# Half of the first output projection in seven-product groups, and two more gate groups behind the last attention head

## The chip, the cores and the metric

The kernel runs on one core of a Trainium2 chip. The time is the device time of one execution of the whole program in microseconds (us); lower is better. The core has a matrix engine (TensorE, PE in the views; its weight loads are listed as PEld), a vector engine (DVE), a scalar engine (ACT), GpSimd (POOL), and the SyncE queue (SP), which here only issues DMAs. ACT and POOL issue some DMAs too. The engines take their own instructions in the order of the program and wait for each other through semaphores.

## The reference

Two transformer blocks in a row on 512 tokens of width 2048, in float32. The part that the change touches is the end of the first block:

```python
zin = rmsnorm(x, gain) @ w_in
q, k, v, g_attn, u, g_pool, m_attn, m_pool = split(zin)
o_attn = stick_breaking_attention(q, k, v) * silu(g_attn)      # 8 heads of 128
o_pool = (multiscale_pool(u) @ pool_w) * pool_scale * silu(g_pool)
merged = sigmoid(m_attn) * (o_attn @ w_attn_up) + sigmoid(m_pool) * (o_pool @ w_pool_up)
hs = x + merged @ w_out                                        # 2048 x 2048
x1 = rmsnorm(hs, final_gain)                                   # enters the second block
```

The second block has two layers, each with sliding-window attention, latent attention and an output projection onto a residual; its first layer begins with a norm of x1.

## The kernel before

**Number format.** Every float32 operand is split into two parts, high and low, in a format that TensorE takes at full rate. A product is three matmuls: high by high, high by low, low by high. Weights come by DMA as chunks of 128x1024 into six buffers `ws`; `ahead` (L175) splits a chunk with one ACT copy (`wh`, L195) and one DVE subtraction (`wl`, L196), up to two chunks ahead of the matmuls.

**Plain units.** `unit` (L380) makes one output tile (128 features x 512 tokens) from its chunks; a chunk is 8 contraction tiles, so 24 matmuls of 512 columns. The up projections `w_au` and `w_pu` take one chunk for each of 16 output tiles, the output projection `w_out` takes two for each of 16. An evacuation function then reads the finished PSUM bank; for `w_out` that is `ev_out` (L837), which adds the residual (read from `xT`), scales by the final gain, stores the tile in DRAM (`xs`), splits it for the next block, and adds its squares to two sums on POOL.

**Groups.** Most of the first block's input projection runs in groups (`products`, L235). A group makes two output tiles from four chunks, and treats weights and tokens as 2x2 blocks, so that seven products p1, p2, q5, p3, p6, p7, q4 do the work of eight. Each product is 24 matmuls of 256 columns (272 where the 16 meta tokens go along) into one of three PSUM regions ga, gb, gc. The sums of weight chunks are made by accumulating DMAs, issued by POOL (L204), three in a group, and one DVE addition (L202); the sums of token blocks are made once, in tiles that stay in SBUF (`XS`). `expand` (L215) writes the order: the last three products p3, p7, q4 of a group run inside the next one; before a `Flush` mark a group ends by itself.

**Heads.** The plan runs over 8 heads. Head h has a group for query and gate and one for key and value. Behind the even heads come a group for pool gates and one for pool inputs, behind the odd ones three "gate groups" (`gate_group`, L767: the merge gates m_attn, m_pool, whose sigmoids are written to DRAM, `smd`, by ACT's queue). Twelve gate groups in all. The attention of a head is a generator (`stick`, L897): pieces of it are issued between the matmuls of later groups. When a piece may come is set by an estimated clock that counts matmuls only: each `yield cost, delay, banks` says after how much estimated time (ns) the next piece may go, and `poll` (L122) lets it in. At its end the generator transposes the values on PE (`pv`, L1000), has ACT and DVE split them (`vh`, L1003, `vl`, L333), waits `yield 5 * 109, 3500, 1` (L1010), and then issues the 15 matmuls `o` (L1019) into the same PE stream. The result goes to DRAM (`oad`).

**Order around the last head.** `reload` (L751) brings attention outputs back from `oad` as tiles `rh`, `rl`: tiles 0 to 2 ahead of the last gate group, tiles 3 to 7 in `attention_done` (L787), which first issues what is left of all generators. Then follow the `w_au` units, whose first one reads all eight tiles. All general tiles share a pool of 77 buffers. SP issues weight loads, reloads and stores in program order.

**Second block.** In its first layer `pre_x` (L1297) loads the residual tiles `xr` one unit ahead and scales each by `rs1` on POOL (L1303).

Of the kernel before, what the change touches and what calls it, by code (L numbers as in the profile page):

```python
# [14 lines left out]
P = 128  # L15
D = 2048
KT = D // P
S = 512
# [50 lines left out]

class Group:  # L70


    def __init__(self, blocks, X, evacs, cols, meta=0):
        self.b, self.X, self.evacs, self.cols, self.meta = blocks, X, evacs, cols, meta


class K:
# [137 lines left out]
    def expand(self, plan):  # L215

        out, left, mid = [], [], []
        for n, u in enumerate(plan):
            if isinstance(u, Group):
                p1, p2, q5, p3, p6, p7, q4 = self.products(u)  # L220
                x3, x7, x4 = [[x] for x in left] or ([], [], [])
                if isinstance(plan[n + 1], Flush):
# [12 lines left out]
    def products(self, g):  # L235
# [7 lines left out]
        st = {}  # L243
# [12 lines left out]
        def product(key, op, region, first, after):  # L256
            c0, c1 = (mid, hi) if op in ("A22", "S1", "S3") else (lom if key in ("p1", "p2", "p3", "p6") else lo, mid)

            def body():
                wh, wl = self.chunk()  # L260
                if first:
                    st[region] = self.bank("g" + region)
                o = st[region][:, c0 - lom:c1 - lom] if c0 < mid else st[region][:, lo - lom:mid - lom]
                mm = nc.tensor.matmul
                nj = len(g.X)
                for part in range(2):
                    for n in range(nj):
                        xh, xl, oh, ol = g.X[n][op]
                        xh, xl = xh[:, oh + c0:oh + c1], xl[:, ol + c0:ol + c1]
                        sl = slice(n * P, n * P + P)  # L270
                        if part == 0:
                            mm(o, wh[:, sl], xh, start=first and n == 0, stop=False, skip_group_check=True)  # L272
                            mm(o, wh[:, sl], xl, start=False, stop=False, skip_group_check=True)  # L273
                        else:
                            mm(o, wl[:, sl], xh, start=False, stop=n == nj - 1, skip_group_check=True)  # L275
                        if n % 4 == 3 or part == 0 and n % 2:
                            yield 4 * 118
                after(st[region])
# [3 lines left out]
        wide = slice(0, mid - lom)  # L282
# [3 lines left out]
        main = slice(lo - lom, mid - lom)  # L286

        def after1(a):
            st["y0"], st["y1"] = self.U("y0"), self.U("y1")
            nc.scalar.copy(st["y0"][:, two], a[:, main])  # L290
            if g.meta:
                nc.scalar.copy(st["y0"][:, hi:hi + g.meta], a[:, :g.meta])

        def after2(a):
            nc.scalar.copy(st["y0"][:, one], a[:, wide])

        def after5(c):
            nc.vector.tensor_tensor(st["y1"][:, two], c[:, main], st["y0"][:, two], ALU.subtract)

        def after6(b):  # L300
            y = st["y1"]
            nc.vector.tensor_tensor(y[:, lo:mid], b[:, main], st["y0"][:, two], ALU.add)
            if g.meta:
                nc.vector.tensor_tensor(y[:, lom:lo], b[:, :g.meta], st["y0"][:, hi:hi + g.meta], ALU.add)

        def after3(c):
            v = st["y1"][:, one]
            nc.vector.tensor_tensor(v, c[:, wide], v, ALU.subtract)

        def after7(b):  # L310
            w = st["y1"][:, two]
            nc.vector.tensor_tensor(w, w, b[:, main], ALU.subtract)  # L312
            g.evacs[1](st["y1"])

        def after4(b):
            nc.vector.tensor_tensor(st["y0"][:, two], b[:, main], st["y0"][:, two], ALU.add)
            g.evacs[0](st["y0"])
# [160 lines left out]
    def build(self):  # L478
        nc, tc, i = self.nc, self.tc, self.i
        with tc.tile_pool(name="cst", bufs=1) as cp, tc.tile_pool(name="wp", bufs=1, reuse_waits="tile") as self.wp, \  # L480
# [16 lines left out]
            self.oad = [self.dp.tile([8, P, S], F32, name=f"oad{n}") for n in range(2)]  # L497
            self.opd = [self.dp.tile([8, P, S], F32, name=f"opd{n}") for n in range(2)]
# [10 lines left out]
    def block1(self, plan):  # L509
# [4 lines left out]
        def load():  # L514
# [27 lines left out]
            def sums():  # L542
# [15 lines left out]
                nc.vector.tensor_scalar(self.trir[:, P:], self.ones, -1.0, None, ALU.mult)  # L558
                yield from self.rms_gen(acc, NT, D, self.rsb, 5000, True)
# [37 lines left out]
        X = self.X  # L597
        XS = self.XS = []
# [152 lines left out]
        def reload(dst, src, ts):  # L751
            def f():
                for t in ts:
                    h, l = dst[t] = self.UR("rh"), self.UR("rl")
# [17 lines left out]
        for g in range(4):  # L772
# [3 lines left out]
            rest.append([x for _ in range(3) for x in gate_group(next(ms_))])  # L776
        rest[7].insert(2, reload(self.oa, self.oad, range(3)))
# [38 lines left out]
        ms = []  # L816

        def ev_yp(n):
            def f(b):
# [5 lines left out]
                h, l = self.UR("mh"), self.UR("ml")  # L825
                self.split(h[:, :S], l[:, :S], t[:, :S])
                ms.append((h, l))
                merged[n] = None
            return f
# [5 lines left out]
        acc = {}  # L835

        def ev_out(n):  # L837
            def f(b):
                if n == 0:
                    self.op.clear()  # L840
                    acc[0], acc[1] = self.U("acc1"), self.U("acc2")
                xr, hs, fg = xres.pop(n), self.U("hs"), self.U("fgx")
                nc.vector.tensor_tensor(hs[:, :S], b, xr[:, :S], ALU.add)
                nc.scalar.activation(fg[:, :S], hs[:, :S], AF.Copy, scale=self.vcol(V_FG, n))
                nc.sync.dma_start(self.xs[0][n], fg[:, :S])
                h, l = self.UR("xh"), self.UR("xl")
                g = self.vcol(V_G0, n)
                nc.scalar.activation(h[:, :S], fg[:, :S], AF.Copy, scale=g)
                nc.vector.scalar_tensor_tensor(l[:, :S], fg[:, :S], g, h[:, :S].bitcast(F32), ALU.mult, ALU.subtract)
                for a, t in ((0, hs), (1, fg)):  # L850
                    sq = self.U("sq")
# [825 lines left out]
```

## Time and profile before

| | |
|---|---|
| runs of the kernel | 2661.83, 2662.19, 2663.93 us; median 2662.19 us |
| the profiled execution | 2662.2 us |
| its span (first to last instruction) | 2660.5 us |
| granted TensorE clock, mean | 0.991 of full |
| PE busy | 2607.5 us, 98% of the span |
| DVE, ACT, POOL busy | 1634.5 us (61%), 1255.3 us (47%), 592.0 us (22%) |

The page gives busy times, the span in 40 slices, the DMA queues, the chain of work that ended last and the costliest groups of instructions. Matmuls overlap, so the time that one adds is the distance from its start to the next one's start, not its own duration. All times in the views are us from the start of the span.

### The profile page before, as it was taken

The page shows a single profiled execution, that of the slowest core. Times are in us where ns is not written, and L with a number is a line of the kernel's source. Part 1 is how long each engine was busy: PE and PEld are TensorE (multiplying, and loading weights), DVE is VectorE, ACT ScalarE, POOL GpSimd, SP SyncE. Part 2 cuts the span into 40 slices and gives each one's busy share as a digit, 9 for nine tenths or more (in the row PEclk, how much of TensorE's full clock was granted, in tenths as well). Part 3 has the DMA queues.
Part 4 walks back from the last instruction along what each step waited for, and adds up shares of the span by engine and source line. Part 5 has one row for each costly group of instructions (what it writes and reads, how often), then busy time and mean ns, then how long its engine had stood idle before and what let it go on. Part 6 is the DMA issues. An engine that isn't in the chain of part 4 may idle for free.

```text
span 2660.5 us, 38650 instructions
## 1 busy us (share of the span) xinstructions
PE 2607.5 (98%) x15038; PEld 2286.7 (86%) x15038; DVE 1634.5 (61%) x2285; ACT 1255.3 (47%) x2195; POOL 592.0 (22%) x664
## 2 busy tenths in 40 slices
PE   8999999999999899999999999999999999999997
PEld 7899999999999878888888888888888888888886
DVE  7667767767767634644566655567455665556734
ACT  6655655654655522233345544444334554434433
POOL 2121122123123100022113321243211332113223
PEclk9999999999999999999999999999999999999998
DMA  5567767776776764444322223323332222232322
GB/s 196 159 157 188 199 166 194 190 172 167 186 182 171 191 237 147 143 138 143 115 97 81 72 80 106 94 74 115 120 124 90 80 76 83 95 105 74 104 95 72
DMA packets 117721, 351.05 MB, mean 132 GB/s; under 512 B 12833, under 2 KB 17441, under 8 KB 117537
## 3 DMA queue, kind: packets, MB, share of 16 engines
q1 hardware_dynamic: 90592, 273.06, 30.8%
q0 software_dynamic: 15552, 56.63, 12.4%
q10 hardware_dynamic: 11392, 18.88, 1.9%
q8 instruction: 118, 1.93, 0.3%
q14 instruction: 67, 0.54, 0.1%
HBM read 319.16 MB, written 29.36 MB: 131 GB/s over the span
## 4 chain that ended last, share of the span: by engine, by line
PE 79%; DVE 6%; ACT 6%; issue 4%; DMA 3%; POOL 1%; ACTq 0%; SPq 0%; DVEq 0%; POOLq 0%
PE pm L353 38%; PE pm L361 19%; ACT wh L195 2%; DVE wl L196 2%; PE s L1534 2%; DMA ws<-w_in 2%; PE gb L272 2%; PE gb L273 2%; PE gb L275 2%; PE ga L275 2%; PE gc L272 1%; PE gc L273 1%; PE gc L275 1%; PE ga L272 1%; PE ga L273 1%
## 5 line engine op out<-in xcount | busy, mean ns | idle before, releaser
L196 DVE TENSOR_TENSOR wl<-ws,wh 128x1024 fp32r<-128x1024 f32 (+3 forms) x549 | 703.3, 1284 | 390.7 <-ACT wh L195 386.1
L195 ACT CAST wh<-ws 128x1024 fp32r<-128x1024 f32 (+3 forms) x549 | 561.3, 1030 | 248.7 <-PE pm L353 110.8
L353 PE MATMUL pm<-xh,wh 128*128 128x512 f32 x1120 | 445.5, 398 | 8.2 <-ACT xh L532 7.5
L353 PE MATMUL pm<-xl,wh 128*128 128x512 f32 x1120 | 441.0, 394 | 0.0
L361 PE MATMUL pm<-xh,wl 128*128 128x512 f32 x1096 | 280.9, 395 | 0.0
L353 PEld LDWEIGHTS pm<-xh,wh 128*128 128x128 f32 x1120 | 210.9, 188 | 58.7 <-ACT xh L532 8.2
L353 PEld LDWEIGHTS pm<-xl,wh 128*128 128x128 f32 x1120 | 210.9, 188 | 48.0 <-DVE xl L533 1.0
L361 PEld LDWEIGHTS pm<-xh,wl 128*128 128x128 f32 x1096 | 202.2, 188 | 43.6
L353 PE MATMUL pm<-yh,wh 128*128 128x512 f32 (+1 forms) x536 | 203.5, 383 | 0.0
L353 PE MATMUL pm<-yl,wh 128*128 128x512 f32 (+1 forms) x536 | 203.1, 382 | 0.0
L204 POOL DMA_DIRECT2D ws<-w_in x108 | 94.4, 908 | 295.1 <-DVE wl L196 187.9
L272 PE MATMUL gb<-xh,wh 128*128 128x256 f32 x576 | 141.9, 284 | 7.7 <-DVE y L312 6.2
L272 PE MATMUL ga<-xh,wh 128*128 128x256 f32 (+1 forms) x576 | 141.6, 284 | 1.9 <-ACT wh L195 1.0
L273 PE MATMUL ga<-xl,wh 128*128 128x256 f32 (+1 forms) x576 | 140.9, 282 | 0.0
L273 PE MATMUL gb<-xl,wh 128*128 128x256 f32 x576 | 140.7, 283 | 0.0
L361 PE MATMUL pm<-yh,wl 128*128 128x512 f32 (+1 forms) x536 | 130.4, 382 | 0.0
L353 PEld LDWEIGHTS pm<-yl,wh 128*128 128x128 f32 x536 | 100.6, 188 | 20.4
L353 PEld LDWEIGHTS pm<-yh,wh 128*128 128x128 f32 x536 | 100.6, 188 | 20.2
L272 PEld LDWEIGHTS gb<-xh,wh 128*128 128x128 f32 x576 | 110.0, 191 | 8.9 <-ACT af L969 5.6
L361 PEld LDWEIGHTS pm<-yh,wl 128*128 128x128 f32 x536 | 96.9, 188 | 19.7
L272 PEld LDWEIGHTS ga<-xh,wh 128*128 128x128 f32 x576 | 108.7, 189 | 2.3 <-ACT wh L195 1.2
L273 PEld LDWEIGHTS gb<-xl,wh 128*128 128x128 f32 x576 | 109.6, 190 | 0.0
(353 smaller groups left out, 5627.6 us busy)
## 6 DMA issues: line engine op xcount, KB each, us to landing
ws<-w_in SPq DMA_DIRECT2D x283, 512.0 KB, 4.0
ws<-w_in POOLq DMA_DIRECT2D x108, 512.0 KB, 6.1
ws<-w_out SPq DMA_DIRECT2D x96, 512.0 KB, 3.9
smd<-sg ACTq DMA_DIRECT2D x32, 256.0 KB, 4.6
ws<-w_au SPq DMA_DIRECT2D x16, 512.0 KB, 4.2
sm<-smd SPq DMA_DIRECT2D x32, 256.0 KB, 4.1
ws<-w_pu SPq DMA_DIRECT2D x16, 512.0 KB, 3.8
xr<-xs SPq DMA_DIRECT2D x32, 256.0 KB, 4.1
```

The source lines that it names most:

```text
L195: self.nc.scalar.copy(h[:, a:b], t[:, a:b])
L196: self.nc.vector.tensor_tensor(l[:, a:b], t[:, a:b], h[:, a:b].bitcast(F32), ALU.subtract)
L204: self.nc.gpsimd.dma_start(x.tile[:, :w], y, accum_op=ALU.add)
L272: mm(o, wh[:, sl], xh, start=first and n == 0, stop=False, skip_group_check=True)
L273: mm(o, wh[:, sl], xl, start=False, stop=False, skip_group_check=True)
L275: mm(o, wl[:, sl], xh, start=False, stop=n == nj - 1, skip_group_check=True)
L353: mm(ps, w[:, sl], x[:, lo:hi], start=s, stop=e)
L361: mm(ps, wl[:, sl], rhs[kt][0][:, lo:hi], start=False, stop=last and n == len(kts) - 1)
L1534: mm(o, p[:, q], r[:, :w], start=x == 0, stop=x == 4)
```

## The change

**The output projection.** Its contraction over 2048 is cut in two. The first half (weights `w_outa`, laid out anew on the host) runs as four groups of seven products; each group makes four output tiles, and a product's 24 matmuls of 256 columns are two sets of 12 (`subs`), one for each half of a PSUM bank. The token operands are the first eight merged tiles; `pair_gen` makes their sums, once, behind the `w_pu` units. The four results go to DRAM (`partd`). The second half (`w_outb`) runs as 16 plain units of one chunk; `pre_part` loads the partial result and the residual back, and `ev_out` adds both. `expand` places the last two `w_pu` units inside the first group, and with the mark `Spread` the last three products of the last group between the first three `w_outb` units. What is kept in DRAM is now the tile ahead of the final gain, and the scaling in the second block (`pre_x`) is one DVE operation with the gain, in place of the POOL one.

**The heads.** The odd heads have 2, 2, 3 and 5 gate groups instead of 3 each. Reloads of attention outputs come ahead of the fourth (tiles 0 to 2) and fifth (tiles 3 to 6) gate group of the last head, and `attention_done` reloads tile 7 alone. The delay between transposes and `o` matmuls is 6000 instead of 3500.

```diff
     def expand(self, plan):
...
+                units = []
+                while not left and len(units) < 2 and out and isinstance(out[-1], Unit):
+                    units.insert(0, out.pop())
+                if units:
+                    u1, u2 = units
+                    out += [p1, u1, p2, q5, u2, p6]
+                elif isinstance(plan[n + 1], Flush):
                     out += [p1, *x3, *x7, *mid, q5, *x4, p6, p3, p7, p2, q4]
...
+            elif isinstance(u, Spread):
+                spread = True
+            elif left and spread and isinstance(u, Unit):
+                out += [u, left.pop(0)]
+                spread = bool(left)
...
-                    for n in range(nj):
+                    for x in range(subs * nj):
+                        q, n = divmod(x, nj)
+                        o = st[region][:, q * hw + r0:q * hw + r0 + c1 - c0]
                         xh, xl, oh, ol = g.X[n][op]
...
-            rest.append([x for _ in range(3) for x in gate_group(next(ms_))])
-        rest[7].insert(2, reload(self.oa, self.oad, range(3)))
+            rest.append([x for _ in range((2, 2, 3, 5)[g]) for x in gate_group(next(ms_))])
+        rest[7].insert(3, reload(self.oa, self.oad, range(3)))
+        rest[7].insert(5, reload(self.oa, self.oad, range(3, 7)))
...
-            reload(self.oa, self.oad, range(3, 8))()
+            reload(self.oa, self.oad, range(7, 8))()
...
+        def part_gen(n, y):
+            yield 0, 2500, 0
+            nc.sync.dma_start(self.partd[n], y[:, :S])
...
+                p, xr = part.pop(n)
+                nc.vector.tensor_tensor(p[:, :S], b, p[:, :S], ALU.add)
+                nc.vector.tensor_tensor(p[:, :S], p[:, :S], xr[:, :S], ALU.add)
+                self.start(out_gen(n, p, n == 0), 1000)
...
+        def out_gen(n, hs, first):
+            yield 0, 0, 0
+            h, l = self.UR("xh"), self.UR("xl")
+            g = self.fg0[:, n:n + 1]
+            nc.scalar.activation(h[:, :S], hs[:, :S], AF.Copy, scale=g)
+            nc.sync.dma_start(self.xs[0][n], hs[:, :S])
+            yield 0, 800, 0
+            nc.vector.scalar_tensor_tensor(l[:, :S], hs[:, :S], g, h[:, :S].bitcast(F32), ALU.mult, ALU.subtract)
...
+        def pre_part(n):
+            def f():
+                for j in ([0, 1, 2] if n == 0 else [n + 2] if n + 2 < KT else []):
+                    part[j] = self.U("part"), self.U("xr")
+                    nc.sync.dma_start(part[j][0][:, :S], self.partd[j])
+                    nc.sync.dma_start(part[j][1][:, :S], i["xT"][j][:, META:])
...
+        cols = (0, S // 2, S)
+        for m in range(4):
+            ev = [tuple(ev_part(4 * m + 2 * q + k) for k in range(2)) for q in range(2)]
+            plan.append(Group([i["w_outa"][m, k] for k in range(4)], ms, ev, cols))
+        plan.append(Spread())
         for n in range(KT):
-            plan.append(self.unit(i["w_out"][n], ms, ev_out(n), pre=pre_x(n)))
+            plan.append(self.unit(i["w_outb"][n], msb, ev_out(n), pre=pre_part(n)))
...
-        yield 5 * 109, 3500, 1
+        yield 5 * 109, 6000, 1
...
-                        nc.gpsimd.tensor_tensor(xr[:, :S], xr[:, :S], self.rs1, ALU.mult)
+                        nc.vector.scalar_tensor_tensor(xr[:, :S], xr[:, :S], self.vcol(V_FG, j), self.rs1, ALU.mult, ALU.mult)
```

Where instructions stand on SP's queue at the end of the attention, before (`oad` holds the attention outputs, `ws` are weight chunks, 13 loads of `w_in` come since the last head's small pool weight):

```order
L172 DMA ws<-w_in 128x1024 x13
L755 DMA rh<-oad_86 128x512
L756 DMA rl<-oad_87 128x512
...
L172 DMA ws<-w_in 128x1024
L172 DMA ws<-w_au 128x1024 x8
L755 DMA rh<-oad_86 128x512
L756 DMA rl<-oad_87 128x512
...
L803 DMA sm<-smd 128x512 x2
```

Three pairs of `rh` and `rl` stand at the first place and five at the second. Of the change, at the same place:

```order
L177 DMA ws<-w_in 128x1024 x18
L806 DMA rh<-oad_86 128x512
L807 DMA rl<-oad_87 128x512
...
L177 DMA ws<-w_in 128x1024 x3
L806 DMA rh<-oad_86 128x512
L807 DMA rl<-oad_87 128x512
...
L177 DMA ws<-w_in 128x1024
L177 DMA ws<-w_au 128x1024 x8
L806 DMA rh<-oad_86 128x512
L807 DMA rl<-oad_87 128x512
L855 DMA sm<-smd 128x512 x2
```

There are three pairs, four pairs and one pair now: seven of the eight reloads stand ahead of the loads of `w_au`, and only the pair of tile 7 behind the eighth of them.

PE's stream at the end of the attention of head 6, before (`pv` are the transposes, `o` the output matmuls, `ga`, `gb`, `gc` regions of a group):

```order
L1001 MATMUL pv_9690<-cst,y_8565 16x128
L272 MATMUL gb<-xh,wh 128x256
...
L275 MATMUL gb<-xh,wl 128x256 x8
...
L273 MATMUL ga<-xl,wh 128x272
L1019 MATMUL o<-sh,vh 128x512
```

and of the change:

```order
L1079 MATMUL pv_9225<-cst,y_8100 16x128
L293 MATMUL gb<-xh,wh 128x256
...
L296 MATMUL gb<-xh,wl 128x256 x8
...
L294 MATMUL ga<-xl,wh 128x272
L296 MATMUL ga<-xh,wl 128x272 x8
...
L294 MATMUL gc<-sl,wh 128x256
L1097 MATMUL o<-sh,vh 128x512
```

Between the transposes and the first `o` stood 32 matmuls of the group; now there are 52: the last 8 of `ga` and the first 12 of `gc` moved ahead of `o`.

## Rows read from the trace of the kernel before

**Rows 1.** The page: the chain that ended last, shares of the span by engine
```profile
PE 79%; DVE 6%; ACT 6%; issue 4%; DMA 3%; POOL 1%; ACTq 0%; SPq 0%; DVEq 0%; POOLq 0%
```

**Rows 2.** By stretch: us, busy us (instructions) by engine, PE clock, DMA share, GB/s
```profile
107.00:892.00 785.00, 770.22 (x6221) 758.63 (x6221) 563.84 (x804) 445.44 (x737) 184.89 (x245) 0.99 0.72 179
200.00:300.00 100.00, 96.70 (x767) 94.53 (x766) 70.30 (x106) 57.18 (x95) 19.91 (x30) 0.98 0.72 183
600.00:700.00 100.00, 97.47 (x766) 95.36 (x765) 74.03 (x107) 54.29 (x91) 26.83 (x35) 0.97 0.67 172
800.00:890.00 90.00, 86.61 (x680) 84.91 (x679) 66.55 (x89) 49.49 (x83) 28.24 (x30) 0.96 0.64 168
890.00:900.00 10.00, 10.00 (x84) 9.71 (x84) 6.52 (x14) 5.92 (x11) 2.84 (x6) 1.00 1.04 263
900.00:990.00 90.00, 76.54 (x396) 63.61 (x395) 39.01 (x56) 31.18 (x46) 2.89 (x6) 0.91 0.65 212
1124.00:1301.00 177.00, 177.00 (x769) 144.00 (x768) 76.75 (x65) 68.27 (x93) 37.25 (x30) 1.00 0.44 143
```

**Rows 3.** PE's timeline, starts of two neighbouring chunks of a `w_out` unit
```profile
1129.54 0.40 PE L353 MATMUL pm<-mh,wh 128*128 128x512 f32 x1
...
1135.07 0.39 PE L353 MATMUL pm<-mh,wh 128*128 128x512 f32 x1
```

**Rows 4.** PE's timeline, the first matmul of a product and the first one behind it
```profile
901.73 0.28 PE L272 MATMUL gc<-sh,wh 128*128 128x256 f32 x1
...
904.56 0.29 PE L964 MATMUL z<-ch,trir 128*128 128x272 f32 x1
```

**Rows 5.** PE's waits, 0 to 900 us, then 900 to 1300: total us, times, longest
```profile
PE o L1019 <- DVE vl L333: 5.9, 6, 2.7
PE o L1019 <- ACT vh L1003: 2.0, 1, 2.0
PE gb L272 <- DVE y L312: 6.2, 2, 5.3
PE pm L353 <- DMA rh<-oad: 3.4, 3, 2.0
PE pm L353 <- DMA rl<-oad: 2.7, 4, 1.4
PE gb L272 <- DVE y L302: 1.2, 1, 1.2
```

**Rows 6.** ACT's timeline in the last group: the store's issue and ACT's wait
```profile
898.16 0.33 ACTq L679 DMA_DIRECT2D smd<-sg  x1
...
904.92 0.60 ACT L926 ACTIVATE spa<-z 128x512 f32<-128x512 f32 x1 [3.48 <-DMA smd<-sg]
```

**Rows 7.** SP's timeline: the second reload's first issue
```profile
933.77 0.38 SPq L755 DMA_DIRECT2D rh<-oad  x1
```

**Rows 8.** DMA issues by kind: count, KB each, median us from issue to landing
```profile
ws<-w_in POOLq DMA_DIRECT2D x108, 512.0 KB, 6.1
rh<-oad SPq DMA_DIRECT2D x8, 256.0 KB, 4.7
rl<-oad SPq DMA_DIRECT2D x8, 256.0 KB, 5.4
```

**Rows 9.** Groups by shape, 107 to 892 us: count, busy us, mean ns
```profile
L196 DVE TENSOR_TENSOR wl<-ws,wh 128x1024 fp32r<-128x1024 f32 x241 | 299.1, 1242 | 163.0 <-ACT wh L195 162.8
L298 DVE TENSOR_TENSOR y<-gc,y 128x256 f32<-128x256 f32 x35 | 14.7, 420 | 7.3 <-PE gc L275 6.6
L272 PEld LDWEIGHTS ga<-xh,wh 128*128 128x128 f32 x552 | 104.2, 189 | 2.3 <-ACT wh L195 1.2 <-ACT y L290 1.1
```

**Rows 10.** Groups by shape in the `w_out` stage, 1106 to 1260 us
```profile
L196 DVE TENSOR_TENSOR wl<-ws,wh 128x1024 fp32r<-128x1024 f32 x28 | 44.1, 1603 | 16.2 <-ACT wh L195 14.7 <-PE pm L361 1.3
L849 DVE SCALAR_TENSOR_TENSOR xl<-fgx,vec,xh 128x512 fp32r<-128x512 f32 x12 | 9.0, 751 | 19.1 <-ACT xh L848 19.1
```

**Rows 11.** POOL's waits, 1700 to 1880 us, in the second block's first layer
```profile
POOL xr L1303 <- DMA xr<-xs: 18.6, 5, 8.6
```

More of the change, by code (lines that the diff above doesn't have):

```diff
@@ L242, in products @@
         b11, b21, b12, b22 = g.b
-        st = {}
+        subs = len(g.evacs)
+        st = {q: {} for q in range(subs)}
         lo, mid, hi = g.cols
@@ L259, in body @@
             def body():
+                if key == "p1" and g.pre:
+                    g.pre()
                 wh, wl = self.chunk()
@@ L273, in body @@
                             mm(o, wh[:, sl], xl, start=False, stop=False, skip_group_check=True)
                         else:
-                            mm(o, wl[:, sl], xh, start=False, stop=n == nj - 1, skip_group_check=True)
-                        if n % 4 == 3 or part == 0 and n % 2:
+                            mm(o, wl[:, sl], xh, start=False, stop=x == subs * nj - 1, skip_group_check=True)
+                        if x % 4 == 3 or part == 0 and x % 2:
                             yield 4 * 118
-                after(st[region])
+                for q in range(subs):
+                    after(st[region][:, q * hw:], st[q], q)
@@ L291, in after1 @@
             if g.meta:
[L292 to L302, printed above, removed]
+                nc.scalar.copy(t["y0"][:, hi:hi + g.meta], a[:, :g.meta])
@@ L308, in after3, with after7 @@
+        def after3(c, t, q):
+            v = t["y1"][:, one]
             nc.vector.tensor_tensor(v, c[:, wide], v, ALU.subtract)
-        def after7(b):
-            w = st["y1"][:, two]
+        def after7(b, t, q):
+            w = t["y1"][:, two]
             nc.vector.tensor_tensor(w, w, b[:, main], ALU.subtract)
[L313 to L317, printed above, removed]
+            g.evacs[q][1](t["y1"])
@@ L597, in block1, with pair_gen @@
         X = self.X
+        def pair_gen(x0, x1, dst, j):
+            yield 0, 0, 0
+            Q = S // 2
+            a, b = self.U("sa"), self.U("sb")
+            ab = lambda t, n: t[:, n * Q:n * Q + Q]
+            tt = nc.vector.tensor_tensor
+            tt(ab(a, 1), ab(x0, 1), ab(x1, 1), ALU.subtract)
+            tt(ab(a, 0), ab(a, 1), ab(x0, 0), ALU.subtract)
+            tt(ab(b, 0), ab(x1, 0), ab(a, 0), ALU.add)
+            tt(ab(x0, 1), ab(x0, 0), ab(x0, 1), ALU.subtract)
+            r = []
+            for src in (x0, x1, a):
+                yield 0, 1500, 0
+                h, l = self.UR("sh"), self.UR("sl")
+                nc.scalar.copy(h[:, :S], src[:, :S])
+                yield 0, 800, 0
+                self.low(l[:, :S], src[:, :S], h[:, :S])
+                r.append((h, l, 0, 0))
+            s4 = self.UR("s4")
+            nc.scalar.copy(s4[:, :Q], ab(b, 0))
+            yield 0, 800, 0
+            self.low(s4[:, Q:S], ab(b, 0), s4[:, :Q])
+            dst[j] = {"A11": r[0], "A12": r[1], "A22": r[1], "S1": r[2], "S2": r[2], "S3": r[0], "S4": (s4, s4, 0, Q)}
         XS = self.XS = []
@@ L824, in f @@
                 nc.vector.tensor_tensor(t[:, :S], t[:, :S], mg[:, :S], ALU.add)
-                h, l = self.UR("mh"), self.UR("ml")
-                self.split(h[:, :S], l[:, :S], t[:, :S])
-                ms.append((h, l))
                 merged[n] = None
+                if n < KT // 2:
+                    mt[n] = t
+                    if n % 2:
+                        self.start(pair_gen(mt[n - 1], t, ms, n // 2), 1500)
+                else:
+                    h, l = self.UR("mh"), self.UR("ml")
+                    self.split(h[:, :S], l[:, :S], t[:, :S])
+                    msb.append((h, l))
             return f
@@ L835, in block1, with ev_part, f @@
         acc = {}
+        part = {}
+        def ev_part(n):
+            def f(y):
+                self.start(part_gen(n, y), 1500)
+            return f
+        def part_gen(n, y):
+            yield 0, 2500, 0
+            nc.sync.dma_start(self.partd[n], y[:, :S])
         def ev_out(n):
```

81 lines of the change are left out of this document (45 added, 36 removed).

## The prediction

> **What bounds the kernel now.** I read the chain that ended last first: 79% of it is PE [rows 1]. Then the stretches: in the output projection PE is busy for all 177 us at full clock, and in the long stretch of groups for 770 of 785 us [rows 2]. So an edit gains only where it takes matmuls away, takes waits from PE, or keeps the granted clock up, and everything on DVE, ACT, POOL and the DMA queues is hidden until it makes PE wait. The third view is therefore the list of PE's waits. Two places stand out: the `o` matmuls of the heads, which wait for the split values (5.9 us for `vl`, 2.0 for `vh`), and the end of the attention, 900 to 1300 us, with 6.2 + 3.4 + 2.7 + 1.2 = 13.5 us [rows 5]. The fourth is the clock. Four stretches were granted 0.98, 0.97, 0.96 and 0.91 of the full clock [rows 2], a mean of times at 2.4 GHz and times at 1.2 GHz; the share that is missing, times the length, is what it cost: 2.0 + 3.0 + 3.6 us in the first three, 8.1 us in the last. In each of them PE had waited just before.
>
> The profiled execution took 2662.2 us (1.7 us of it outside the span), which is the median of the runs shown. All sums start there. About 0.2%, or 5.3 us, is what a measurement can tell from no change.
>
> **The projection's matmuls.** In a plain unit the starts of two neighbouring chunks are 1135.07 - 1129.54 = 5.53 us apart, so 24 matmuls of 512 columns cost 230 ns each [rows 3]. The first half of the contraction is one such chunk for each of 16 output tiles: 16 x 5.53 = 88.5 us go. In their place come 4 groups of 7 products. A product of the same size (24 matmuls of 256 columns) took 904.56 - 901.73 = 2.83 us, 118 ns each [rows 4], so 28 x 2.83 = 79.2 us come: **9.3 us gained**, before waits.
>
> One rule speaks against this. TensorE: Matmul & The Clock Gate of the Trainium skill, section Back-to-back issue gap, says that in a stream of load and matmul pairs the spacing is set by both, about 131 ns at 512 columns and 81 ns at 128. An estimate of mine between the two (about 98 ns at 256) makes the 672 new matmuls 66 us and the 384 old ones 50 us, a loss of 16 us, and the sum below 2654 us instead of 2629. The trace does not agree: its spacings, 230 and 118 ns, go by columns.
>
> What hides the rest of the new stage? DVE in a group of 7 x 2.83 = 19.8 us: 7 splits of 1.24 us, one addition like them, and 10 evacuations of 0.42 us for two sets [rows 9], 14.1 us. In a plain unit of 5.53 us: a split of 1.6 us at most, one scaled split of 0.75 us [rows 10], and two additions that I take at the same 0.75: 3.9 us. ACT and POOL are lighter than now in the long stretch of groups. The sums of `pair_gen` fall into the `w_pu` stage and are due only some 8 units later. DMA is closer: a group moves 7 chunks of 0.52 MB (three of them accumulate) and stores four results of 0.26 MB, 4.7 MB in 19.8 us, or 238 GB/s. The groups now run at 179 GB/s with a DMA share of 0.72; a stretch at share 1.04 moved 263 GB/s [rows 2]. So about nine tenths of what the engines do, and accumulating DMAs, 6.1 us to land now [rows 8], will take longer. PE has two chunks of lead (5.7 us). I put **2 us** of waits here, between 0 and 18.
>
> DMA: Bandwidth & Descriptors of the Trainium skill, section Bandwidth, has some 358 GB/s for a core's HBM traffic, which would leave a third of the queue free; the trace shows 1.04 of it taken at 263 GB/s.
>
> **The delay ahead of `o`.** By the order 20 more matmuls stand between transposes and `o`: 20 x 0.118 = 2.4 us. The longest wait, 2.7 us, shrinks to 0.4, the one for `vh` of 2.0 leaves perhaps as much for `vl` behind it, and the others (0.4 to 1.1 us) go: of 7.9 us **7.1 are gained**. The clock was low right behind the three longest of them. If they caused it, 8.6 us come back; waits of about 1 us stand elsewhere without it, so I take **6 us**, between 0 and 8.6. What is late next is the head's store, which has over a group to spare.
>
> **The end of the attention.** Now 13.5 us of waits and 8.1 us of clock, 21.6 us. Where does it come from? The 5.3 us wait starts with ACT, which waited 3.5 us because its next tile was still being stored [rows 6] while reloads filled the DMA queue (890 to 900, [rows 2]); DVE came late behind it. Then the first `w_au` unit waits for reloads that SP issued from 933.77 on [rows 7], 10 of them. After the change head 7's `o` stands 12.5 products ahead of `w_au`, seven tiles are issued within the groups, and one pair remains. That pair still sits behind the eighth `w_au` load on SP, so it is issued about when the last product ends, and lands 4.7 and 5.4 us later [rows 8]; the unit needs it after 14 matmuls, 3.2 us. That is 2 us of wait. I keep 2.1 us of the short waits for DVE in the flushed group, 2 us of clock, and 3 us for the two bursts of 6 and 8 reloads on the queue, which now have weight loads behind them. 21.6 - 9.1 = **12.5 us gained**, between 0 and 21.6.
>
> **Fewer gate groups behind the early heads.** The same twelve groups, the same pieces of attention; those of the odd heads run under the next head's groups. I take 0, between -3 and +3: PE had under 2% idle there in the stretch of groups [rows 2]. **Scaling on DVE in the second block.** 16 operations of 0.75 us, and a wait that sat on POOL (18.6 us in five, [rows 11]) can now sit on DVE with a weight split queued behind it. The splits run two chunks, 11 us, ahead, so 0; without that cover 4 us.
>
> **Sum.** 2662.2 - 9.3 + 2 - 7.1 - 6 - 12.5 = **2629 us**. With every gain full: 2662.2 - 9.3 - 7.9 - 8.6 - 21.6 = 2615.
>
> **Rivals.**
> *DMA is late in the projection's groups.* For it: 238 GB/s against 179. If the last three groups run at today's pace, 4.7 MB at 179 GB/s is 26 us instead of 19.8, some 19 us in all: 2629 - 2 + 19 = 2646. Against it: 263 GB/s was reached.
> *The end of the attention doesn't get shorter,* because the reloads wait on SP for tiles of the pool of 77 and hold up the weight loads behind them, which they didn't at their old place. The 12.5 us are not gained: 2642.
> *The delay does not do what it says:* DVE's queue is what is late, and slides along. Neither 7.1 nor 6 us come: 2642.
> *Slower than before: the clock.* If PE waits again and again in the projection's groups and is granted 1.2 GHz there, each product takes twice its 2.83 us: up to 79 us more, 2708. It decides from 39 us on (2629 + 39 = 2668), about half of the stage. For it: low clock behind waits of 2 us and more. Against it: in 785 us of groups the clock was 0.99 [rows 2].
> *Slower: the weight load sets the spacing.* Each load lasts 189 ns [rows 9]; if the new matmuls took that instead of 118 ns, 672 x 0.189 = 127 us against 88.5, and 2629 + 9.3 + 38.5 = 2677. The same loads stand in today's groups at 118 ns. By the issue-gap rule above, the trace disagrees as well.
>
> **Chances.** Forecast 0.62 (its own range 2620 to 2638); late DMA 0.14; the attention's end 0.10; the delay 0.06; clock 0.05; weight load 0.01; nothing that can be told from before, through several of these, 0.02. The range 2616 to 2648 takes in the full gains and the three middle rivals, and leaves out some 0.15. Faster than 2656.9: 0.62 + 0.14 + 0.10 + 0.06 less 0.01 for late DMA that reaches further = 0.91; the same 0.03; slower 0.06.
>
> **What would show it.** In the profile after: a product of the projection's groups at 2.83 us with no waits between; `o` matmuls without waits above 0.5 us, and the clock at 1.00 in the stretches of heads 0, 4 and 6; the first `w_au` unit waiting once, for the last `rh`; `xr` on DVE without a PE wait in the second block. It is wrong if PE's list shows waits for `wh` in the projection's groups, if the clock falls there, or if the flushed group still waits for a store.

## The result and the profile after

The changed kernel took 2633.84 us (median of 4 runs, 2632.29 to 2637.99) beside 2662.01 for the kernel before: a ratio of 0.9898, 95% interval 0.9886 to 0.9910. Repeated later beside some of its variants it took 2637.42 us, 0.9904 (0.9889 to 0.9918). The profiled execution took 2633.37 us, with a span of 2631.7 us and a mean granted clock of 0.996. The forecast was 2629 in a range of 2616 to 2648.

The stretches first, as in [rows 2]: us, busy us (instructions) by engine, then the granted clock, the DMA share and GB/s. The last two lines lie in the projection: groups of products, then half units.

```profile
200.00:300.00 100.00, 97.94 (x787) 95.82 (x786) 73.70 (x111) 57.69 (x96) 20.33 (x30) 1.00 0.74 187
600.00:700.00 100.00, 98.91 (x821) 97.83 (x820) 72.38 (x105) 62.19 (x103) 18.30 (x29) 1.00 0.80 210
800.00:890.00 90.00, 88.78 (x733) 87.47 (x732) 64.91 (x98) 54.97 (x91) 16.94 (x27) 1.00 0.81 215
890.00:990.00 100.00, 93.29 (x498) 79.68 (x497) 40.17 (x50) 31.36 (x38) 0.86 (x1) 0.98 0.73 247
1090.00:1180.00 90.00, 90.00 (x693) 86.79 (x693) 58.16 (x78) 36.70 (x49) 9.49 (x11) 1.00 0.82 216
1180.00:1290.00 110.00, 110.00 (x505) 90.69 (x504) 65.03 (x83) 52.48 (x74) 45.32 (x32) 1.00 0.67 218
```

The three stretches of the heads that had 0.98, 0.97 and 0.96 of the clock now have 1.00, at 2.4 GHz throughout. In the projection PE is busy all the time. DVE has 58.16 of 90 us there and the DMA engines a share of 0.82, neither of them full. The ends of three neighbouring products of a projection group, in PE's timeline:

```profile
1131.48 1.11 PE L296 MATMUL gb<-sh,wl 128*128 128x256 f32 x8
1134.32 1.11 PE L296 MATMUL ga<-sh,wl 128*128 128x256 f32 x8
1137.15 1.11 PE L296 MATMUL gc<-s,wl 128*128 128x256 f32 x8
```

They are 2.84 and 2.83 us apart. PE's waits over the whole program (total us, times, longest), to be read beside [rows 5]:

```profile
PE gb L293 <- ACT wh L200: 6.6, 9, 1.1
PE pm L374 <- DMA rh<-oad: 3.2, 1, 3.2
...
PE gc L293 <- ACT wh L200: 2.6, 2, 2.0
PE t L1648 <- POOL p L1638: 2.5, 1, 2.5
PE gb L293 <- DVE y L333: 1.3, 1, 1.3
...
PE o L1097 <- DVE vl L354: 0.3, 1, 0.3
```

The `o` matmuls waited 7.9 us before and wait 0.3 now. The first `w_au` unit waits once, for the last `rh`. Two waits are new: `gc` for `wh` (2.6 us, 2.0 of them at a product q5 that is followed below), and `t`, transposes of attention probabilities in the second block.

**Where the time went.** Three events divide both traces: the first `w_au` matmul, the column sums `pms` of the next norm, and the end. PE's timeline at the first two, before and then after:

```profile
936.52 0.51 PE L353 MATMUL pm<-rh,wh 128*128 128x512 f32 x1
1312.25 0.40 PE L438 MATMUL pms<-ach,trir 128*128 128x512 f32 x1
...
918.24 0.39 PE L374 MATMUL pm<-rh,wh 128*128 128x512 f32 x1
1280.44 0.39 PE L459 MATMUL pms<-ach,trir 128*128 128x512 f32 x1
```

The first `w_au` matmul starts at 918.24 us (before 936.52): 18.3 us less. From there to `pms` it is 362.2 us (before 375.7): 13.5 us less, 6.0 of them in the first `w_au` unit. From `pms` to the end it is 1351.3 us (before 1348.3): 3.0 us **more**. Together 28.8 us, the difference of the spans.

The loss in the second block can be followed backwards through three engines (start us, duration, and in brackets the idle time before and what ended it). One line each of DVE, DVE, POOL and PE, in order of time, and in a second fence the stretch around the wait, in the columns of the stretches above:

```profile
1691.74 0.75 DVE L1381 SCALAR_TENSOR_TENSOR xr<-xr,vec,rs 128x512 f32<-128x512 f32 x1 [3.91 <-DMA xr<-xs]
...
1699.39 0.17 DVE L1634 RECIPROCAL sm<-sm 128x4 f32<-128x4 f32 x1
...
1699.73 3.27 POOL L1638 TENSOR_SCALAR p<-p,sm 128x512 f32<-128x512 f32 x4 [23.78 <-DVE sm L1634]
...
1702.60 1.65 PE L1648 MATMUL t<-cst,p 128*128 128x128 f32 x10 [2.46 <-POOL p L1638]
```

```profile
1700.00:1708.00 8.00, 5.42 (x22) 4.23 (x22) 5.08 (x9) 2.35 (x7) 4.85 (x7) 0.79 0.17 50
```

The scaling of `xr` stands on DVE right behind the issue of its transfer, so DVE sits 3.91 us until that has landed. Behind it in DVE's queue wait a weight split, then the masks and maxima of the scores, then the reciprocal. POOL can normalise only then, PE's transposes wait 2.46 us for POOL, and the clock in the 8 us around is 0.79, another (1 - 0.79) x 8 = 1.7 us. Before, the same wait for the transfer sat on POOL [rows 11], and the masks on DVE did not stand behind it.

What is left at the end of the attention, in order of time: ACT's split that is late, the product q5 and the one behind it on PE, four reloads on SP, and the first `w_au` unit:

```profile
895.82 1.04 ACT L200 CAST wh<-ws 128x1024 fp32r<-128x1024 f32 x1 [3.82 <-DMA ws<-w_in]
...
896.91 0.39 PE L293 MATMUL gc<-sh,wh 128*128 128x256 f32 x1 [2.02 <-ACT wh L200]
901.32 0.36 PE L293 MATMUL gb<-xh,wh 128*128 128x256 f32 x1 [1.32 <-DVE y L333]
...
884.26 0.32 SPq L806 DMA_DIRECT2D rh<-oad  x1
891.61 0.32 SPq L807 DMA_DIRECT2D rl<-oad  x1
896.08 0.32 SPq L806 DMA_DIRECT2D rh<-oad  x1
899.95 0.32 SPq L807 DMA_DIRECT2D rl<-oad  x1
...
919.02 0.38 SPq L806 DMA_DIRECT2D rh<-oad  x1
...
924.85 0.50 PE L374 MATMUL pm<-rh,wh 128*128 128x512 f32 x1 [3.22 <-DMA rh<-oad]
```

Four of the reloads are issued 4 to 7 us apart. SP's and ACT's transfers tell of their landing on eight semaphores, used in turn, and none of the 726 in this trace is issued before the last one on its semaphore has landed. These four come 0.06 to 0.08 us behind such a landing: a load of `w_in` (884.20), a gate store (891.54) and the two stores of head 7 (896.01, 899.87). So SP is held up there, as the prediction's second rival had it, but by these times it waits for transfers under way and not for tiles of the pool. The gain came all the same. Tile 7 is issued at 919.02, behind all eight `w_au` loads. The waits of this place are 2.02 + 1.32 + 3.22 us, and the clock in the stretch (0.98 over 100 us) costs 2.0: 8.6 us where 21.6 stood before. The low clock lies behind the last of them:

```profile
926.00:929.50 3.50, 3.50 (x10) 2.71 (x10) 0.13 (x1) 1.04 (x1) 0.00 (x0) 0.52 0.68 248
```

(1 - 0.52) x 3.5 = 1.7 us at half the clock, 1.2 GHz, where PE had just waited 3.22.

### The profile page after: what moved, and what is told of

The parts are those of the page before. It is cut to its first block, busy times and chain, and to the rows that moved or that the text cites. A ratio compares the mean times of both kernels' runs of the same rounds, so it can differ in the third digit from the quotient of the medians.

```text
span 2631.7 us, 39404 instructions
## 1 busy us (share of the span) xinstructions
PE 2588.4 (98%) x15326; PEld 2287.6 (87%) x15326; DVE 1682.6 (64%) x2398; ACT 1266.6 (48%) x2215; POOL 586.8 (22%) x660
## 3 DMA queue, kind: packets, MB, share of 16 engines
q1 hardware_dynamic: 95200, 281.45, 31.8%
q8 instruction: 120, 1.97, 0.3%
## 4 chain that ended last, share of the span: by engine, by line
PE 78%; DVE 6%; ACT 5%; DMA 5%; issue 4%; POOL 1%; ACTq 0%; SPq 0%; DVEq 0%; POOLq 0%
PE pm L374 36%; PE pm L382 18%; DMA ws<-w_in 4%; PE gb L293 2%; PE gb L294 2%; PE gb L296 2%; ACT wh L200 2%; DVE wl L201 2%; PE ga L293 2%; PE ga L296 2%; PE ga L294 2%; PE s L1612 1%; PE gc L293 1%; PE gc L296 1%; PE gc L294 1%
## 5 line engine op out<-in xcount | busy, mean ns | idle before, releaser
L200 ACT CAST wh<-ws 128x1024 fp32r<-128x1024 f32 (+3 forms) x561 | 575.8, 1032 | 295.2 <-PE pm L374 117.0
L1175 POOL TENSOR_TENSOR gs<-p,sg 128x512 f32<-128x512 f32 x32 | 41.5, 1297 | 300.9 <-ACT sg L495 300.9
```

The lines of the kernel that those rows point to most:

```text
L200: self.nc.scalar.copy(h[:, a:b], t[:, a:b])
L1175: nc.gpsimd.tensor_tensor(gs[:, :S], p[:, :S], e[:, :S], ALU.mult)
```

## The experiments

Each was compared with runs of the kernel before on the same chip, taken in turn with them. Kernels that were run together, in one series, are told together.

### One part of the change at a time, and the residual

`d_delay` is the kernel before with the delay alone:

```diff
-        yield 5 * 109, 3500, 1
+        yield 5 * 109, 6000, 1
```

> The kernel before with one part of the change alone: the delay ahead of the `o` matmuls is 6000 instead of 3500. Theory of the prediction: the `o` matmuls' waits for `vl` and `vh` go (7.9 us of PE's list) and with them the low clock behind the three longest, 13 us by the prediction's two terms, up to 16 by the comparison of the two traces: 2646 to 2649 us. Rival 1, the waits go but the low clock has another cause: 2654. Rival 2, DVE's queue slides along and nothing is gained: 2662, with the waits still in PE's list.

`d_heads` is the kernel before with the gate groups, the reloads and `attention_done` of the change (a line by which a reload first has its head's attention issued is not shown):

```diff
-            rest.append([x for _ in range(3) for x in gate_group(next(ms_))])
-        rest[7].insert(2, reload(self.oa, self.oad, range(3)))
+            rest.append([x for _ in range((2, 2, 3, 5)[g]) for x in gate_group(next(ms_))])
+        rest[7].insert(3, reload(self.oa, self.oad, range(3)))
+        rest[7].insert(5, reload(self.oa, self.oad, range(3, 7)))
...
-            reload(self.oa, self.oad, range(3, 8))()
+            reload(self.oa, self.oad, range(7, 8))()
```

> The kernel before with the end of the attention alone: gate groups 2, 2, 3, 5 behind the odd heads, reloads of tiles 0 to 2 and 3 to 6 within the last groups, tile 7 at the end; the delay stays at 3500 and the projection plain. Theory of the prediction: 12.5 us, 2649.5 us. By the comparison of the two traces about 9: 2653, with one wait of some 3 us for the last `rh` and low clock behind it left. Rival, the reloads wait on SP for tiles and hold the weight loads up, so that nothing is gained: 2662.

`d_proj` is the changed kernel with those two edits taken back, so the projection and what follows it in the second block.

> The kernel before with the projection alone (28 products and 16 half units in the place of 16 whole ones, the residual scaled on DVE in the second block); delay, gate groups and reloads as before. Theory of the prediction: 9.3 us of matmuls less 2 of waits and nothing lost in the second block, 2655. By the comparison of the two traces 8.5 us are gained in the projection and 3.5 to 4 lost in the second block: 2657 to 2658. Rival, the low clock and the wait in the second block come from the other parts of the change: 2653 to 2654.

`a_xr` is the changed kernel with this edit:

```diff
         def ev_wa(n):
             def f(b):
                 xr = xres.pop(n)
+                if l == 0:
+                    nc.vector.scalar_tensor_tensor(xr[:, :S], xr[:, :S], self.vcol(V_FG, n), self.rs1, ALU.mult, ALU.mult)
...
                     nc.sync.dma_start(xr[:, :S], self.xs[l][j])
-                    if l == 0:
-                        nc.vector.scalar_tensor_tensor(xr[:, :S], xr[:, :S], self.vcol(V_FG, j), self.rs1, ALU.mult, ALU.mult)
```

> The changed kernel, but the residual of the second block is scaled on DVE just ahead of the addition that uses it, a unit or more after its transfer was issued, and no longer right behind that issue. Theory: in the changed kernel DVE sat 3.9 us until `xr` had landed, with the masks of the scores queued behind it; POOL's normalisation and PE's transposes came late by it (2.5 us), and the clock behind that cost 1.7: 4.2 us come back, 2629.6. Rival 1, only the wait comes back: 2631.3. Rival 2, DVE is full there with or without the transfer: 2633.8, and PE still waits for `p`.

| kernel | median us | runs | ratio to before (2662.04 us) | 95% interval |
|---|---|---|---|---|
| d_delay | 2650.35 | 5 | 0.9960 | 0.9948 to 0.9973 |
| d_heads | 2653.17 | 5 | 0.9965 | 0.9953 to 0.9978 |
| d_proj | 2657.05 | 11 | 0.9983 | 0.9974 to 0.9992 |
| a_xr | 2631.30 | 4 | 0.9888 | 0.9873 to 0.9903 |

The three parts alone gain 11.7, 8.9 and 5.0 us, 25.6 in all, and the whole change 28.2 in its first measurement (2662.01 - 2633.84) and 26.0 in its second, told below: they add up within what these runs can tell.

PE's waits in `d_delay`:

```profile
PE gb L272 <- DVE y L312: 6.4, 2, 5.5
...
PE gc L272 <- ACT wh L195: 2.3, 3, 1.2
...
PE o L1019 <- DVE vl L333: 0.3, 1, 0.3
```

The `o` matmuls wait 0.3 us, and the clock is 1.00 in all three of the stretches 200 to 300, 600 to 700 and 800 to 890 us. Nothing but the delay was changed, so the low clock of these stretches came with the waits. Of the rivals, "waits without clock" (2654) falls by the clock in these stretches and "nothing" (2662) by the time, which is 1.4 us above the theory's range. By these rows 7.6 us of waits and 8.6 of clock are won, 16.2; the profile has 11.9. Waits of 2.3 us for `wh` come on, in groups of the heads at 620, 648 and 851 us. The product that waits for `y` at the end of the attention starts 10.5 us earlier than before (900.10 and 910.62 us), the first `w_au` matmul 10.8 (925.75) and `pms` 10.0 (1302.24); the last 1.9 us come in the second block, where nothing was changed. So the delay is worth some 10 to 11 us ahead of that product, and what else is missing of the 16.2, beside those 2.3, is not placed. At the end of the attention the wait for `y` stays, and the stretch has somewhat less clock (0.91 before):

```profile
890.00:990.00 100.00, 87.44 (x432) 72.22 (x432) 42.66 (x60) 33.91 (x48) 2.87 (x6) 0.90 0.69 227
```

By the positions of the first `w_au` matmul and of `pms` (10.8 and 10.0 us earlier) this place gives back under 1 us.

In `d_heads` it is the other way round: `rh` and `rl` cost 2.7 us in place of 6.1 and no product waits for DVE's `y`, but the `o` matmuls wait even longer than before.

```profile
PE o L1022 <- DVE vl L333: 6.6, 8, 2.8
...
PE o L1022 <- ACT vh L1006: 3.1, 2, 2.0
PE gc L272 <- ACT wh L195: 1.9, 1, 1.9
PE pm L353 <- DMA rh<-oad: 1.9, 1, 1.9
```

`d_proj` has the wait for `p` (2.9 us) that the whole change has, so it comes with this part and not with the heads. In `a_xr` that wait is gone from PE's list, and the transposes start without idle time before them. DVE's two next scalings and PE's transposes there:

```profile
1686.03 0.75 DVE L1370 SCALAR_TENSOR_TENSOR xr<-xr,vec,rs 128x512 f32<-128x512 f32 x1 [0.80 <-DMA xr<-xs]
1696.66 0.72 DVE L1370 SCALAR_TENSOR_TENSOR xr<-xr,vec,rs 128x512 f32<-128x512 f32 x1
...
1701.35 1.25 PE L1648 MATMUL t<-cst,p 128*128 128x128 f32 x10
```

The chain transfer, DVE, POOL, PE is therefore shown; rival 2 falls. The time, 2631.30, is that of rival 1, by which only the wait comes back, but the clock came back too: it is 1.00 from 1696 to 1710 us. The size is not sharp by the times (2.5 us against the first measurement of the changed kernel, in another series); the profiles of all kernels give it further below.

### The reloads spread, both edits, and the projection by itself

`a_rel` takes the burst of reloads of four tiles and the last pair apart; a reload with `later = k` is issued k products further on (the loop in `expand` that does it is not shown):

```diff
-        rest[7].insert(5, reload(self.oa, self.oad, range(3, 7)))
+        for t, k in ((7, 8), (6, 5), (5, 3), (4, 1), (3, 0)):
+            f = reload(self.oa, self.oad, range(t, t + 1))
+            f.later = k
+            rest[7].insert(5, f)
...
             self.need(*list(self.gens))
-            reload(self.oa, self.oad, range(7, 8))()
```

> The changed kernel, but the reloads of tiles 3 to 7 are spread over the products of the last two groups (3 after the fourth gate group, then 1, 3, 5 and 8 products later), so that tile 7 stands ahead of the last two of the eight `w_au` loads on SP, and SP does not hold four reloads in one burst. Theory: the first `w_au` unit's wait for the last `rh` (3.2 us) and the low clock behind it (1.7) go, and with the burst of four the wait of 2.0 for `wh` behind it: 2627 to 2629 us. Rival 1, the single reloads each wait for a tile of the pool and hold up a weight load each: 2634 or more, with waits for `wh` in the flushed group. Rival 2, the low clock comes from the short waits of the flushed group: 2630.6.

`a_both` has the edits of `a_rel` and `a_xr`; `after_again` is the changed kernel as it is; `d_proj_xr` is `d_proj` with the edit of `a_xr`.

> The changed kernel with both edits: reloads 3 to 7 spread, and the residual of the second block scaled just ahead of its use. Theory: the two are in different blocks and add up: 4.9 to 6.9 us from the reloads and 2.5 to 4.2 from the residual, 2623 to 2626.5 us. Rival, the reloads spread hold up the weights: 2631, as with the residual alone.

> The changed kernel as it is, beside its variants on the same chip: 2633.8 us by every theory.

> The kernel before with the projection alone, and the residual of the second block scaled on DVE just ahead of its use. Theory: the projection is worth the 8 to 9 us of its matmuls, and all that its single run lacked was lost in the second block: 2653 to 2654 us. Rival, the projection itself gains only some 5 us and the second block nothing: 2657, as without this edit.

| kernel | median us | runs | ratio to before (2663.46 us) | 95% interval |
|---|---|---|---|---|
| after_again | 2637.42 | 4 | 0.9904 | 0.9889 to 0.9918 |
| a_rel | 2630.40 | 4 | 0.9881 | 0.9865 to 0.9897 |
| a_both | 2625.92 | 4 | 0.9862 | 0.9848 to 0.9876 |
| d_proj_xr | 2652.10 | 5 | 0.9959 | 0.9945 to 0.9973 |

The changed kernel came out 3.6 us above its first measurement, so a few us are told only within a series. There `a_rel` is 7.0 us ahead of it and `a_both` 11.5, a version that beats both kernels. The residual alone is worth 2.5, 4.5 and 5.0 us in three pairs (changed kernel and `a_xr`, `a_rel` and `a_both`, `d_proj` and `d_proj_xr`; the first and last pair across series). `d_proj_xr` answers the question on the projection: its profile has a span of 2651.3 us, 9.2 less than before, and its runs are 11.4 us below those of the kernel before. Of the 9.2, 8.2 lie ahead of `pms` (1304.10, before 1312.25). What `d_proj` lacked was lost in the second block: behind `pms` its profile takes 1353.0 us and that of `d_proj_xr` 1347.2.

In `a_rel` the first `w_au` unit no longer waits for `rh`, and the clock is 1.00 there. But the product q5 still waits:

```profile
PE gc L300 <- ACT wh L200: 2.7, 2, 2.2
```

2.2 us with single reloads, 2.0 with the burst: the burst is not what makes those weights late, that step of the expectation was wrong, and the time is 1.4 us above its range.

### What makes q5's weights late

The DMA view of the changed kernel for 884 to 900 us, when q5's weights are on their way, has this by queue (packets, MB, share of the 16 engines' time) and by issue (count, KB each, median us to landing):

```profile
q0 software_dynamic: 545, 1.97, 63.3%
q1 hardware_dynamic: 846, 1.56, 28.3%
...
ws<-w_in POOLq DMA_DIRECT2D x2, 512.0 KB, 13.3
```

The first queue is POOL's, and all transfers on it accumulate. They take 63 of 105 parts of the engines' time (the share in these 16 us is 1.05) and land after 13.3 us, where the median over the kernel before was 6.1 [rows 8]. Three kernels ask whether the reloads matter to that. `a_oldreload` is the changed kernel with the old place of five reloads:

```diff
-        rest[7].insert(5, reload(self.oa, self.oad, range(3, 7)))
...
-            reload(self.oa, self.oad, range(7, 8))()
+            reload(self.oa, self.oad, range(3, 8))()
```

> The changed kernel with the gate groups where it has them, but the reloads of tiles 3 to 7 all behind the last product, as before; only tiles 0 to 2 are reloaded within the groups. Theory: what the reloads within the groups are worth is the stall of the first `w_au` unit: ten reloads stand behind eight `w_au` loads on SP, and the waits of before for `rh` and `rl` (6.1 us) and 3 to 5 us of low clock come back, 2639 to 2643 us beside 2634 to 2637 for the changed kernel. Rival, the move of the gate groups is all that counts: no difference.

`a_late` is `a_both` with later reloads. `a_noreload` is `a_both` without five of them; it leaves out that part of the result, since the up projection reads tiles 0 to 2 in the place of 3 to 7:

```diff
-        for t, k in ((7, 8), (6, 5), (5, 3), (4, 1), (3, 0)):
+        for t, k in ((7, 8), (6, 7), (5, 6), (4, 5), (3, 4)):
```

> The kernel with both edits, but the five single reloads stand 4, 5, 6, 7 and 8 products behind the fourth gate group, so that none is issued ahead of the product `q5` whose weights come late in the flushed group. Theory: that product's wait (2.0 to 3.4 us in the four profiles) comes from accumulating transfers that land late (13.3 us instead of 6.3) while the DMA share is above 1.04, and reloads and `w_au` loads share it; with less on the queue there the wait shrinks to under 1.5 us and the clock stays up behind it: 2622 to 2624 us. Rival 1, the accumulations alone fill the queue (63 of 104 parts of it) and the wait stays: 2626. Rival 2, the reloads are now too late for the first `w_au` unit: 2630.

```diff
                 for t in ts:
+                    if dst is self.oa and t > 2:
+                        dst[t] = dst[t - 3]
+                        continue
```

> The kernel with both edits, without the reloads of tiles 3 to 7: the first units of the up projection read tiles 0 to 2 in their place, so that this part of the result is left out. It tells what all five reloads cost, wherever they stand. Theory: the wait ahead of `q5` goes or shrinks under 1 us and no clock is lost behind it, 2620 to 2623 us. Rival, the wait stays at 2 us or more, since the accumulating transfers and the stores of the gates fill the queue by themselves: 2625 to 2626.

| kernel | median us | runs | ratio to before (2662.21 us) | 95% interval |
|---|---|---|---|---|
| a_oldreload | 2639.83 | 5 | 0.9914 | 0.9900 to 0.9927 |
| a_late | 2625.66 | 4 | 0.9864 | 0.9851 to 0.9878 |
| a_noreload | 2625.86 | 4 | 0.9863 | 0.9850 to 0.9877 |

`a_oldreload` is 2.4 to 6.0 us behind the changed kernel (its two measurements, in other series, with intervals that overlap its own). Its first `w_au` unit takes 16.1 us (919.63 to 935.76), beside 10.9 in the changed kernel, so the place of the reloads is worth some 2 to 6 us. By difference the move of the gate groups has the rest of the 8.9 us of `d_heads`; it was not run alone. `a_late` and `a_noreload` are no faster than `a_both`, as their rivals had it. Without any reload of tiles 3 to 7 the same stretch of `a_noreload` reads, by engine and then by DMA queue:

```profile
884.00:900.00 16.00, 14.56 (x124) 14.36 (x124) 8.11 (x11) 7.67 (x11) 2.28 (x3) 1.00 1.04 263
```

```profile
q0 software_dynamic: 571, 2.09, 66.2%
q1 hardware_dynamic: 355, 1.30, 23.5%
...
ws<-w_in POOLq DMA_DIRECT2D x3, 512.0 KB, 11.0
```

The share is 1.04 all the same, nearly two thirds of it accumulations: these transfers of the last two groups, with weight loads and stores beside them, fill the engines by themselves. q5 still waits 1.4 us. Over all profiles of the changed kernel and its variants, one of each, its wait is 1.8 to 3.4 us where reloads stand ahead of it (`a_xr`, the changed kernel 2.0, `a_rel`, `after_again`, `a_both`), and 0.8 to 1.7 where none of tiles 3 to 7 does (`a_oldreload`, `a_noreload`, `a_late`). So the reloads seem to add some 1 us to this wait, and about half of it (1.3 of 2.5 us in the mean) stays without them. In the time of `a_late` and `a_noreload` even that does not show, but their intervals are some 4 us wide to either side. That fewer accumulations would end the wait was not tried.

## Why the prediction was right, point by point

**The projection's matmuls (9.3 us).** Right in mechanism and size: products are 2.83 to 2.84 us apart. From the projection's first matmul to `pms` the profile after takes 190.4 us (1090.05 to 1280.44), with two `w_pu` units of 5.57 us in it; that leaves 179.3 where 188.3 stood (1123.99 to 1312.25), 9.0 us gained. What I had not foreseen: the `w_pu` units themselves now start 5.57 us apart, 5.47 before, without a wait between them, some 1.5 us over the sixteen. Why is open.

**Waits of DMA there (2 us, up to 18).** None came: PE was busy for all of 1090 to 1290 us, at a DMA share of 0.82 and 216 GB/s in the groups. The rival "DMA is late" falls, and with full clock and a spacing of 2.84 us so do the two slower ones. The issue-gap rule of the Trainium skill (TensorE: Matmul & The Clock Gate, Back-to-back issue gap) would have made this part a loss. The trace after does not agree with it either: 2.84 us for 24 matmuls of 256 columns are 118 ns each.

**The delay (7.1 us of waits and 6 of clock).** `d_delay` measured 11.7 for the 13.1, and some 10 to 11 us by the positions in its trace. Both halves are shown: 7.6 us of waits went, and the clock came back to 1.00 in the three stretches without another edit. Of the clock I had counted 6 of 8.6 us; there it came back in full. What I had not counted is that waits for `wh` of 2.3 us come on.

**The end of the attention (12.5 us).** `d_heads` alone measured 8.9. In the whole change 8.6 us are left at this place, where the prediction kept 9.1, but of other things: 3.2 us and 1.7 of low clock for the last pair (I had 2 and 2), and not 3 us for bursts of reloads but 2.0 for weights summed by accumulating transfers. For the changed kernel the reading that the reloads fill the DMA queue was too narrow: without five of them the share stays at 1.04; for the kernel before it was not tried. The 21.6 us that stood there counted too much clock. In its two stretches of half clock PE was busy for 11.2 of 17.1 us and waited for the rest:

```profile
908.16:915.00 6.84, 4.38 (x20) 4.41 (x21) 5.73 (x11) 3.42 (x6) 1.82 (x5) 0.50 0.23 78
942.29:952.53 10.24, 6.80 (x12) 3.66 (x13) 1.23 (x1) 1.25 (x2) 0.00 (x0) 0.50 0.87 305
```

Time in which PE waits costs no clock, so the low clock cost 11.2 / 2 = 5.6 us there and not 8.1.

**The second block (0 us; 4 without cover).** This is the step that failed. I wrote that the splits run two chunks ahead and would cover a wait on DVE. They do cover the split; but I named only the split as queued behind it. The masks of the scores stand there too, and POOL's normalisation and PE's transposes hang on them with no such lead. From `pms` to the end the loss is 3.0 us, and 2.5 and 1.7 us by the wait and the clock behind it, close to the bound named for the case without cover. The other profiles bear it out. The five with the scaling right behind the issue (the changed kernel twice, `d_proj`, `a_rel`, `a_oldreload`) take 1350.9 to 1353.0 us from `pms` to the end and have a wait of 2.5 to 3.1 us for `p`; the five with the scaling at its use (`a_xr`, `a_both`, `d_proj_xr`, `a_late`, `a_noreload`) take 1346.4 to 1348.8 and have none. The means are 4.3 us apart.

**The sum.** Before `pms` the prediction had 32.9 us of gains and the traces have 31.8: 25.6 and 24.3 up to the second `w_au` unit (953.40 us before, 929.13 after), 7.3 and 7.5 from there on. That the second pair agrees is luck: 2 us of waits did not come, and some 1.5 in the `w_pu` units came in their place. With the 3.0 us lost behind `pms`, 28.8 are left. So the 4.4 us between 2629 and the profiled 2633.4 are mostly the term of the second block.

## What to carry to other kernels

When an operation with a wait on a transfer moves to another engine, list everything that stands behind it in that engine's queue, and follow each to the matrix engine; the lead of one of them covers only that one. Give a transfer a unit of time before the operation that reads it is issued, rather than scaling a tile right behind its load. A short wait of the matrix engine may cost as much again in clock, so removing it pays up to double. And when a transfer is late, ask the DMA view which queue takes the engines' time before moving the transfers that are easy to move.

## What the runs showed of the hardware

**The queue of accumulating transfers took more of the DMA engines per byte than the queue of plain loads.** In the changed kernel, 884 to 900 us, 63.3% went for 1.97 MB of POOL's accumulations and 28.3% for 1.56 MB of SP's plain loads: 32 and 18 parts per MB, a factor of 1.8. Over the whole program before, it was 12.4% for 56.63 MB and 30.8% for 273.06 MB, a factor of 1.9. The two queues differ in the issuing engine too (the first is a software queue, the second a hardware one), and no run has plain transfers on POOL's queue, so the accumulation itself is not told apart from the queue. It is the whole queue that the row shows, so its landing time of 13.3 us is that of a full queue. Full queues moved at different rates: at a share of 1.04 `a_noreload` moved 263 GB/s, and `a_rel`, between 915 and 920 us, without accumulations and with 1.79 of 2.05 MB on SP's queue of loads, moved 411:

```profile
915.00:920.00 5.00, 5.00 (x43) 4.88 (x42) 3.26 (x6) 3.12 (x5) 0.00 (x0) 1.00 1.04 411
```

DMA: Bandwidth & Descriptors of the Trainium skill, section Bandwidth, puts the ceiling of the ports at about 435 GB/s and that of a core's HBM traffic at about 358; the 411 lies above the second and below the first.

**A wait does not always cost clock.** In the changed kernel the wait of 2.46 us for `p` was followed by low clock (0.79 in 8 us). In `a_rel` the same matmuls waited a little longer, and the clock stayed at 1.00 before and behind (PE's timeline, then two stretches):

```profile
1697.05 1.66 PE L1657 MATMUL t<-cst,p 128*128 128x128 f32 x10 [2.53 <-POOL p L1647]
```

```profile
1690.00:1700.00 10.00, 7.34 (x37) 5.71 (x36) 7.37 (x18) 6.27 (x19) 3.27 (x4) 1.00 0.28 91
1700.00:1708.00 8.00, 8.00 (x49) 7.08 (x48) 7.90 (x10) 3.54 (x7) 6.46 (x6) 1.00 0.18 50
```

Likewise q5's wait of 3.38 us in `a_both` was followed by 0.62 (897 to 903.5 us), and its 2.02 us in the changed kernel by 1.00; but 1.76 us in `a_xr` were followed by 0.66 (898 to 903 us). What decides between the two in waits of this size, these runs don't tell.
